# Preparing the weight tiles of seven-product pairs one pair ahead, in a two-layer streaming encoder

## The chip, the cores and the metric

The kernel runs on one core of one Trainium2 chip. The metric is the device time in microseconds (us) of one execution. The engines are TensorE (PE, with PEld for its weight loads), VectorE (DVE), ScalarE (ACT), GpSimd (POOL) and SyncE (SP, which here only issues DMA transfers). POOL computes a little and issues the transfers that add their source to their destination.

## The reference, cut to what matters

An encoder of two layers works on 576 tokens (512 of a prompt, 64 of a sample) of width 1024. Each layer is a feed-forward sub-layer, a token mixer and a second feed-forward sub-layer. Every sub-layer reads a norm whose shift and scale, and writes a residual whose gate, come from a conditioning vector `c`:

```python
for l in range(DEPTH):
    mod = (cond @ ada_w[l] + ada_b[l]).reshape(b, N_SUB, 3, D_MODEL)
    shift, scale, gate = mod[:, :, 0], mod[:, :, 1], mod[:, :, 2]
    hh = _modulated_norm(x, norm_g[l, 0], shift[:, 0], scale[:, 0])
    x = x + 0.5 * gate[:, 0, None] * _swiglu(hh, ff_w_in[l, 0], ff_w_out[l, 0])
    ...  # token mixer: gated delta rule and short convolution (l = 0), stick-breaking attention (l = 1)
    hh = _modulated_norm(x, norm_g[l, 2], shift[:, 2], scale[:, 2])
    x = x + 0.5 * gate[:, 2, None] * _swiglu(hh, ff_w_in[l, 1], ff_w_out[l, 1])

def _swiglu(h, w_in, w_out):
    gate, up = jnp.split(h @ w_in, 2, axis=-1)
    return (jax.nn.silu(gate) * up) @ w_out
```

`w_in` is 1024 x 5632 and `w_out` 2816 x 1024, all in float32. The four feed-forward sub-layers are called f0 to f3 here, the two mixers mixer 0 and mixer 1. The order is f0, mixer 0, f1, f2, mixer 1, f3.

## The kernel before

**Products in three matmuls.** Every operand is split into a high part (rounded to the matmul's float32r type) and a low part (what is left). A product is three matmuls: high x high, high x low, low x high. Activations lie in `XH`/`XL` (the sub-layer's input) and `HH`/`HL` (the hidden units), weights in `wh`/`wl`. Tokens are worked on in two halves of 288 columns.

**Weights** come from HBM in tiles of up to 128 x 1024 into a ring of three buffers named `stage`. ACT copies a tile to `wh`, and DVE (or POOL) writes `wl` = tile - `wh`. In other places `wl` is made without DVE: ACT writes `-wh` to `wl`, and a transfer issued by POOL adds the tile to it (`acc_dma`). `wh` and `wl` are rings of four buffers of 128 x 1024.

**Pairs.** A pair is one tile of gate and one of up columns (128 columns each). A plain pair takes 96 matmuls (2 tiles x 8 x 3 x 2 halves). In f1, f2 and f3 the last 16 of the 22 pairs are done with seven products of half-size blocks in place of eight (`dense7`): 84 matmuls, in seven steps of 12, in the order P1, P2, P6, P5, P7, P3, P4. P1, P6, P7 and P4 add to one PSUM bank, and ACT or DVE reads it between them, so that P6 cannot start before ACT has copied what P1 left (`sg`), nor P7 before the copy after P6. Each such pair needs four weight tiles:

- tile 0 (128 x 1024, the loaded tile `st[i, 0]` itself), for P1 and P2,
- tile 1 (128 x 1024, sums of loaded blocks made by DVE in `ss`), for P6 and P5,
- tile 2 (128 x 1024, more sums in `ss`), for P7 and P3,
- tile 3 (128 x 512, a loaded block), for P4.

`w_sum` makes the sums (four DVE operations a pair), `w_tile` calls `w_split` on one of the four. P5, P6, P7 and P4 also need sums of activation blocks, `TH`/`TL`, which `t_task` makes once a sub-layer: four ACT copies, a chain of eight adding transfers on POOL's queue, and four ACT and four DVE operations at its end.

**Order of the work.** Every engine takes its instructions in the order in which the program writes them. `dense7` writes, after the matmuls of each step, the work for other engines (`evac` and the `n ==` lines below them): sums and tiles of the next pair, too. Around them generators (`t_task`, `norm`, the attention's tasks and `ada_task`) are stepped when their due time has passed on a modelled clock (`Model`, `Sched`), so a constant in the model moves what is written where. `ada_task` makes the shift, scale and gate values: for each tile of `ada_w` a load of 512 KB (`aw`) and two DVE operations (`jk`), one tile every so many modelled ns. In f1 and f2 it has 48 tiles to do, every 11000 ns; in mixer 1 24 tiles, every 12000 ns, and the last step of mixer 1 (`last_pairs`) is written only after all of them (`S.finish(at)`).

**Where a sub-layer begins**, `start_sub` runs its first two pairs with the matmuls of both interleaved, while the norm of the second token half is still being made; `mid()` is called between the halves. Plain pairs 2 to 5 follow, then the seven-product pairs 6 and 7 and the first part of the `w_out` products; pairs 8 to 15 and the second part; pairs 16 to 21 and the last part.

Each instruction is recorded through one helper (line 191) or, for adding transfers, line 560, so the profile's groups are told apart by the names of their tiles.

## Time and profile before

| | |
|---|---|
| median of 3 runs | 2574.02 us (2572.0 to 2576.96) |
| the profiled execution | 2568.52 us, span 2566.8 us |
| PE busy | 2385.5 us (93%), mean granted clock 0.960 |
| DVE busy | 1702.3 us (66%) |
| ACT busy | 1050.9 us (41%) |
| POOL busy | 453.7 us (18%) |
| adding transfers to `wl` | 32 of 512 KB from `ss`, 32 of 256 KB from `stage` |

The page names PE as the busy engine, so what counts are the stretches in which it waits. PE matmuls are pipelined: one lasts some 300 ns, and at full clock one starts every 0.132 us. An idle time stands in square brackets with the instruction or transfer that ended it. "Landing" of a transfer is counted from the start of its issue to the arrival of its data.

### The profile page before, as it was taken

The page shows a single profiled execution, that of the slowest core. Times are in us where ns is not written, and L with a number is a line of the kernel's source. Part 1 is how long each engine was busy: PE and PEld are TensorE (multiplying, and loading weights), DVE is VectorE, ACT ScalarE, POOL GpSimd, SP SyncE. Part 2 cuts the span into 40 slices and gives each one's busy share as a digit, 9 for nine tenths or more (in the row PEclk, how much of TensorE's full clock was granted, in tenths as well). Part 3 has the DMA queues.
Part 4 walks back from the last instruction along what each step waited for, and adds up shares of the span by engine and source line. Part 5 has one row for each costly group of instructions (what it writes and reads, how often), then busy time and mean ns, then how long its engine had stood idle before and what let it go on. Part 6 is the DMA issues. An engine that isn't in the chain of part 4 may idle for free. (4 is left out here: it accounts for less than half of the span.)

```text
span 2566.8 us, 46156 instructions
## 1 busy us (share of the span) xinstructions
PE 2385.5 (93%) x18508; PEld 2301.0 (90%) x18508; DVE 1702.3 (66%) x3344; ACT 1050.9 (41%) x2090; POOL 453.7 (18%) x693
## 2 busy tenths in 40 slices
PE   7999999999998988989899999999999959899998
PEld 5999999988888988889899999999888849899998
DVE  7666666697875756686775546455777866648575
ACT  4322222533222433352544446264555535325352
POOL 4000000432222310010122001013334324000001
PEclk8999999998978999999999999999999979999999
DMA  6444443321112275574746446352333323623322
GB/s 234 159 155 147 155 150 118 115 81 51 46 49 90 84 199 161 139 200 150 198 139 165 117 103 161 94 143 85 126 118 120 98 85 123 165 84 98 99 81 81
DMA packets 108794, 318.84 MB, mean 124 GB/s; under 512 B 26226, under 2 KB 28530, under 8 KB 108324
## 3 DMA queue, kind: packets, MB, share of 16 engines
q1 hardware_dynamic: 95044, 273.02, 32.3%
q0 software_dynamic: 13536, 42.87, 9.1%
q8 instruction: 146, 2.39, 0.4%
q14 instruction: 68, 0.56, 0.1%
HBM read 261.47 MB, written 11.51 MB: 106 GB/s over the span
## 5 line engine op out<-in xcount | busy, mean ns | idle before, releaser
L191 PE MATMUL d<-XH,wh 128*128 128x288 f32 x2736 | 841.4, 308 | 52.5 <-DVE x L191 22.3
L191 PE MATMUL d<-XL,wh 128*128 128x288 f32 x2736 | 824.4, 301 | 11.4 <-POOL XL L191 9.9
L191 PE MATMUL d<-XH,wl 128*128 128x288 f32 x2736 | 822.6, 301 | 2.4 <-DVE wl L191 2.4
L191 PEld LDWEIGHTS d<-XH,wh 128*128 128x128 f32 x2736 | 528.2, 193 | 61.7 <-issue 26.2
L191 PEld LDWEIGHTS d<-XL,wh 128*128 128x128 f32 x2736 | 528.2, 193 | 23.4 <-POOL XL L191 16.3
L191 PEld LDWEIGHTS d<-XH,wl 128*128 128x128 f32 x2736 | 527.6, 193 | 3.8 <-DVE wl L191 3.5
L191 DVE TENSOR_TENSOR wl<-stage,wh 128x1024 fp32r<-128x1024 f32 (+3 forms) x287 | 331.1, 1159 | 193.4 <-ACT wh L191 191.7
L191 ACT ACTIVATE wh<-stage 128x1024 fp32r<-128x1024 f32 (+3 forms) x393 | 333.2, 867 | 247.4 <-PE d L191 229.2
L191 PE MATMUL d<-HH,wh 128*128 128x288 f32 x1408 | 416.4, 296 | 1.1 <-ACT HH L191 1.1
L191 PE MATMUL d<-HL,wh 128*128 128x288 f32 x1408 | 416.1, 296 | 0.1
L191 PE MATMUL d<-HH,wl 128*128 128x288 f32 x1408 | 414.2, 294 | 0.0
L191 DVE SCALAR_TENSOR_TENSOR jk<-aw,cb 128x1024 bf16<-128x1024 f32 x272 | 340.5, 1252 | 15.3 <-DMA aw<-in_ada 10.5
L191 DVE SCALAR_TENSOR_TENSOR x<-d,mod,x 128x64 f32<-128x64 f32 (+2 forms) x384 | 146.5, 412 | 227.8 <-PE d L191 227.0
L191 PE MATMUL d<-TH,wl 128*128 128x288 f32 x768 | 232.8, 303 | 44.0 <-DMA wl<-ss 44.0
L191 PEld LDWEIGHTS d<-HH,wh 128*128 128x128 f32 x1408 | 264.2, 188 | 1.3 <-ACT HH L191 1.3
L191 PEld LDWEIGHTS d<-HL,wh 128*128 128x128 f32 x1408 | 264.3, 188 | 1.0 <-DVE HL L191 1.0
L191 PEld LDWEIGHTS d<-HH,wl 128*128 128x128 f32 x1408 | 264.6, 188 | 0.0
L191 PE MATMUL d<-TH,wh 128*128 128x288 f32 x768 | 229.5, 299 | 6.6 <-ACT sg L191 6.6
L191 PE MATMUL d<-TL,wh 128*128 128x288 f32 x768 | 229.6, 299 | 0.0
L191 POOL TENSOR_TENSOR acc<-acc,sq 128x288 f32<-128x288 f32 x72 | 58.4, 811 | 847.9 <-ACT sq L191 847.3
L191 PEld LDWEIGHTS d<-TH,wl 128*128 128x128 f32 x768 | 147.5, 192 | 50.4 <-DMA wl<-ss 50.4
L191 ACT ACTIVATE HH<-hm 128x288 fp32r<-128x288 f32 x176 | 73.5, 442 | 253.4 <-DVE hm L191 252.6
(321 smaller groups left out, 3333.4 us busy)
## 6 DMA issues: line engine op xcount, KB each, us to landing
stage<-in_w SPq DMA_DIRECT2D x301, 512.0 KB, 3.6
aw<-in_ada SPq DMA_DIRECT2D x136, 512.0 KB, 3.7
wl<-ss POOLq DMA_DIRECT2D x32, 512.0 KB, 4.7
stage<-in_w SPq DMA_DIRECT2D x36, 384.0 KB, 3.1
TL<-XL POOLq DMA_DIRECT2D x18, 576.0 KB, 9.4
wl<-stage POOLq DMA_DIRECT2D x32, 256.0 KB, 5.2
TL<-XH POOLq DMA_DIRECT2D x6, 576.0 KB, 9.4
TL<-TL POOLq DMA_DIRECT2D x6, 576.0 KB, 5.6
```

The costliest lines, as they stand in the source:

```text
L191: r = real(*args, **kw)
```

## The change

Six edits:

1. In `dense7` tile 0 of the next pair is written after step P1 (it was after P5), tile 1 after P5 (was after P3), tile 2 after P3 (was after P4). Tile 3 of the running pair stays after P1 and is now always the only one left to do there, but for the first pair of a row, which still makes its tile 2 at that place.
2. Tile 3 gets its own buffers `wh3` and `wl3` (one each, 128 x 512), so a pair takes three of the four buffers of the ring and not all four.
3. Where adding transfers make `wl` (f1 and f2), they do it for tiles 0 and 3, which are loaded data. Tile 2, a sum, is now subtracted on DVE, as tile 0 was. The counts stay: 32 of 512 KB and 32 of 256 KB.
4. `t_task` is spawned in `mid()`, that is between the two halves of a sub-layer's first two pairs, and not behind them.
5. The model has a clock of its own for adding transfers (`ACC`, at 130 in place of 150 GB/s) beside that of the loads. `ada_task` in mixer 1 takes 8500 ns a tile and not 12000.
6. To make room, the ring `hf` of the norms has four buffers and not five, and `dynamic_dma_scratch_size` is 1024 and not 2048.

```diff
-        self.t = {"PE": 0.0, "DVE": 0.0, "ACT": 0.0, "POOL": 0.0, "SP": 0.0, "DMA": 0.0}
+        self.t = {"PE": 0.0, "DVE": 0.0, "ACT": 0.0, "POOL": 0.0, "SP": 0.0, "DMA": 0.0, "ACC": 0.0}
...
     def w_split(i, src, E=V, by_dma=False):
         n = Model.size(src)
-        h, l = wsp.tile([P, 1024], F32R, name="wh"), wsp.tile([P, 1024], F32R, name="wl")
+        if n == HB:
+            h, l = (wsp.tile([P, HB], F32R, name=m, bufs=1) for m in ("wh3", "wl3"))
+        else:
+            h, l = wsp.tile([P, 1024], F32R, name="wh"), wsp.tile([P, 1024], F32R, name="wl")
...
         if n == 0:
-            w_split(i, st[i, 0])
+            w_split(i, st[i, 0], by_dma=S2M[0])
         if n == 1:
             w_split(i, ss[i, 1])
         if n == 2:
-            w_split(i, ss.pop((i, 3)), by_dma=S2M[0])
+            w_split(i, ss.pop((i, 3)))
...
             if n == 0:
-                while len(wt[i]) < 4:
-                    if len(wt[i]) == 2:
-                        w_sum(i, 4)
-                    w_tile(i, len(wt[i]))
+                if len(wt[i]) < 3:
+                    w_sum(i, 4)
+                    w_tile(i, 2)
+                w_tile(i, 3)
             if nxt7:
                 for k in {1: (1,), 2: (2,), 4: (3, 4)}.get(n, ()):
                     w_sum(i + 1, k)
-                k = {3: 0, 5: 1, 6: 2}.get(n)
+                k = {0: 0, 3: 1, 5: 2}.get(n)
                 if k is not None:
                     w_tile(i + 1, k)
...
         nc.gpsimd.dma_start(out, in_, accum_op=OP.add)
         M.issue("POOL", [out], [in_], 1000.0)
-        M.t["DMA"] = max(M.t["DMA"], M.t["POOL"] + 1300.0) + 4.0 * P * Model.size(out) / 150.0
-        M.mark([out], [in_], M.t["DMA"] + 700.0, "POOL")
+        M.t["ACC"] = max(M.t["ACC"], M.t["POOL"] + 1300.0) + 4.0 * P * Model.size(out) / 130.0
+        M.mark([out], [in_], M.t["ACC"] + 700.0, "POOL")
...
-            u = pool.tile([P, 288], F32, name="hf", bufs=5)
+            u = pool.tile([P, 288], F32, name="hf", bufs=4)
...
-    def start_sub(task, evacs):
+    def start_sub(task, evacs, after=None):
 
         def mid():
             S.finish(task[1])
             hold[0] = False
+            if after:
+                after()
...
-                        start_sub(task, [ev0, evac])
-                    tt = S.spawn(t_task(pool)) if PLAIN[2 * l + s // 2] < 22 else None
+                        start_sub(task, [ev0, evac], lambda: tt.append(S.spawn(t_task(pool))))
                 elif seven(pos[0]):
                     if tt:
-                        S.finish(tt)
-                        tt = None
+                        S.finish(tt.pop())
...
-        at = S.spawn(ada_task(mp, [(1, j) for j in (5, 6, 7)], 12000.0, 1))
+        at = S.spawn(ada_task(mp, [(1, j) for j in (5, 6, 7)], 8500.0, 1))
...
-    nc = _bacc.Bacc("TRN2", target_bir_lowering=False, num_devices=1, dynamic_dma_scratch_size=2048)
+    nc = _bacc.Bacc("TRN2", target_bir_lowering=False, num_devices=1, dynamic_dma_scratch_size=1024)
```

**Place 1: a seven-product pair in f1, on ACT.** First ACT's order before, from the `up` copy (after P7) of one pair to the `hm` copy (after P5) of the next. `wh<-ss x2` and `wl<-ss` are tile 1 and tile 2, `wh<-stage 128x512` and its `wl` are tile 3; the first `sg<-d` is the copy after P1.

```order
L191 ACTIVATE up<-d 128x288
L191 ACTIVATE wh<-ss 128x512 x2
L191 ACTIVATE sg<-sg 128x288
L191 ACTIVATE wh<-ss 128x512 x2
L191 ACTIVATE wl<-ss 128x1024
L191 ACTIVATE sg<-d 128x288
L191 ACTIVATE wh<-stage 128x512
L191 ACTIVATE wl<-stage 128x512
L191 ACTIVATE HH<-hm 128x288 x2
L191 ACTIVATE sg<-d 128x288
L191 ACTIVATE hm<-d 128x288
```

And the same piece of the changed kernel (its numbered names are `wh3` and `wl3`):

```order
L191 ACTIVATE up<-d 128x288
L191 ACTIVATE wh<-ss 128x512 x2
L191 ACTIVATE sg<-sg 128x288
L191 ACTIVATE sg<-d 128x288
L191 ACTIVATE wh_11700<-stage 128x512
L191 ACTIVATE wl_11701<-stage 128x512
L191 ACTIVATE wh<-stage 128x512 x2
L191 ACTIVATE wl<-stage 128x1024
L191 ACTIVATE HH<-hm 128x288 x2
L191 ACTIVATE sg<-d 128x288
L191 ACTIVATE hm<-d 128x288
```

Tile 2's three ACT operations are gone from ahead of the copy after P1, and the next pair's tile 0 now stands between tile 3 and `HH`. On DVE the same pairs hold, before, two `ada_w` tiles a pair (`jk,mod`), and in the changed kernel one. Before:

```order
L191 TENSOR_TENSOR ss<-ss,stage 128x512
L191 TENSOR_TENSOR wl<-stage,wh 128x1024
L191 SCALAR_TENSOR_TENSOR jk,mod<-aw,cb 128x1024 x2
L191 TENSOR_TENSOR ss<-stage 128x512
L191 TENSOR_TENSOR ss<-stage,ss 128x512
L191 TENSOR_TENSOR up<-hm,up 128x288
L191 TENSOR_TENSOR sg<-d,sg 128x288
L191 TENSOR_TENSOR wl<-ss,wh 128x1024
L191 SCALAR_TENSOR_TENSOR jk,mod<-aw,cb 128x1024 x2
L191 TENSOR_TENSOR hm<-sg,up 128x288
```

In the changed kernel:

```order
L191 TENSOR_TENSOR ss<-ss,stage 128x512
L191 TENSOR_TENSOR wl<-ss,wh 128x1024
L191 SCALAR_TENSOR_TENSOR jk,mod<-aw,cb 128x1024 x2
L191 TENSOR_TENSOR ss<-stage 128x512
L191 TENSOR_TENSOR ss<-stage,ss 128x512
L191 TENSOR_TENSOR up<-hm,up 128x288
L191 TENSOR_TENSOR sg<-d,sg 128x288
L191 TENSOR_TENSOR wl<-ss,wh 128x1024
L191 TENSOR_TENSOR hm<-sg,up 128x288
```

So it is with most pairs of f1: the modelled clock runs slower per pair, and the `ada_w` tiles spread into the first pairs of f2. In four pairs of f1 the one tile stands where it stands here, between `wl` of tile 1 and the sums; in the others it stands elsewhere in the pair.

**Place 2: DVE where f1 enters its first seven-product pair.** `TL<-TL,TH` are the four last operations of `t_task`. Before:

```order
L191 TENSOR_TENSOR TL<-TL,TH 128x1152
L191 SCALAR_TENSOR_TENSOR jk,mod<-aw,cb 128x1024 x2
L191 TENSOR_TENSOR TL<-TL,TH 128x1152
L191 TENSOR_TENSOR hm<-sg,d 128x288
L191 TENSOR_TENSOR HL<-hm,HH 128x288
L191 TENSOR_TENSOR wl<-stage,wh 128x1024
L191 TENSOR_TENSOR hm<-sg,d 128x288
L191 TENSOR_TENSOR HL<-hm,HH 128x288
```

In the changed kernel:

```order
L191 TENSOR_TENSOR TL<-TL,TH 128x1152
L191 TENSOR_TENSOR hm<-sg,d 128x288
L191 TENSOR_TENSOR HL<-hm,HH 128x288
L191 TENSOR_TENSOR wl<-stage,wh 128x1024
L191 SCALAR_TENSOR_TENSOR jk,mod<-aw,cb 128x1024 x2
L191 TENSOR_TENSOR hm<-sg,d 128x288
L191 TENSOR_TENSOR HL<-hm,HH 128x288
L191 TENSOR_TENSOR ss<-stage 128x512
L191 TENSOR_TENSOR ss<-ss,stage 128x512
L191 TENSOR_TENSOR TL<-TL,TH 128x1152
```

The second `TL` operation has moved behind two token halves' worth of `hm` and `HL`; the transfers that it waits for are written earlier, too (edit 4).

**Place 3: DVE at the end of mixer 1**, from the last split of the attention's output to the residual of `last_pairs`. Before:

```order
L191 TENSOR_TENSOR XL<-so,XH 128x288 x6
L191 SCALAR_TENSOR_TENSOR jk,mod<-aw,cb 128x1024 x8
L191 TENSOR_TENSOR mod<-mod,small 128x16
L191 SCALAR_TENSOR_TENSOR mod<-mod,small 128x16
L191 TENSOR_TENSOR wl<-stage,wh 128x768 x2
L191 SCALAR_TENSOR_TENSOR x<-d,mod,x 128x288 x8
```

In the changed kernel:

```order
L191 COPY wt_23039<-a 64x128
L191 TENSOR_TENSOR XL<-so,XH 128x288 x6
L191 TENSOR_TENSOR wl<-stage,wh 128x768 x2
L191 SCALAR_TENSOR_TENSOR x<-d,mod,x 128x288 x8
```

The last four `ada_w` tiles, which stood ahead of the residual, have moved forward among the attention's work; the last of the 24 now stands ahead of the last attention pair's scans.

More of the change, by code (lines that the diff above doesn't have):

```diff
@@ L802, in ffn @@
         spool[0] = pool
-        tt = None
+        tt = []
         late = {}
@@ L880, in ffn @@
                     else:
-                        start_sub(task, [ev0, evac])
-                    tt = S.spawn(t_task(pool)) if PLAIN[2 * l + s // 2] < 22 else None
+                        start_sub(task, [ev0, evac], lambda: tt.append(S.spawn(t_task(pool))))
                 elif seven(pos[0]):
                     if tt:
-                        S.finish(tt)
-                        tt = None
+                        S.finish(tt.pop())
                     dense7(evac7(jj))
```

## The prediction

> **What bounds the kernel now.** PE is the busy engine, so I first read who makes it wait (columns: us in total, times, longest):
>
> ```profile
> PE d L191 <- DMA wl<-ss: 44.0, 26, 6.8
> PE d L191 <- DVE x L191: 22.3, 2, 19.7
> PE d L191 <- ACT wh L191: 15.6, 3, 7.3
> ```
>
> All three belong to this change: tile 2's adding transfer, the residual at the end of mixer 1, and the entry into the seven-product pairs. What they cost in full is read from stretches between the starts of P1, in the view by windows (us; then busy us and count of PE, PEld, DVE, ACT, POOL; clock; DMA share; GB/s). Three rows each for f1, f2 and f3: pairs 6 and 7 with the first `w_out` part, pairs 8 to 15 with the second, pairs 16 to 20; then six pairs of f3:
>
> ```profile
> 968.58:1053.13 84.55, 76.52 (x554) 75.84 (x553) 54.38 (x94) 25.47 (x45) 3.44 (x4) 0.94 0.47 144
> 1053.13:1217.73 164.60, 145.81 (x1059) 143.47 (x1057) 125.67 (x221) 73.97 (x144) 13.80 (x16) 0.98 0.64 179
> 1217.73:1286.91 69.18, 60.13 (x422) 58.85 (x421) 53.94 (x96) 39.30 (x82) 8.67 (x10) 0.95 0.72 189
> 1428.35:1505.81 77.46, 75.02 (x555) 74.78 (x554) 34.10 (x58) 25.12 (x43) 3.48 (x4) 0.98 0.37 102
> 1505.81:1653.92 148.11, 142.09 (x1058) 140.37 (x1057) 78.56 (x136) 73.28 (x144) 13.82 (x16) 1.00 0.50 129
> 1653.92:1716.99 63.07, 58.57 (x422) 57.40 (x421) 37.02 (x64) 40.25 (x84) 8.62 (x10) 0.97 0.60 144
> 2230.74:2307.12 76.38, 74.03 (x555) 73.33 (x553) 42.84 (x73) 22.11 (x39) 0.00 (x0) 1.00 0.28 83
> 2307.12:2447.14 140.02, 140.02 (x1058) 140.02 (x1057) 91.97 (x152) 61.66 (x128) 0.00 (x0) 1.00 0.30 91
> 2447.14:2502.81 55.67, 55.67 (x422) 55.67 (x421) 44.12 (x73) 32.09 (x72) 0.00 (x0) 1.00 0.30 93
> 2318.25:2385.05 66.80, 66.80 (x506) 66.80 (x505) 54.96 (x92) 39.88 (x90) 0.00 (x0) 1.00 0.31 95
> ```
>
> f3 is the yardstick: 66.80/6 = 11.13 us a pair, PE never idle, a step 11.13/7 = 1.59 us. Its second stretch less six pairs (140.02 - 66.80) is 73.2, the floor of the first. Over the floor lie: f1 11.3 + 24.6 + 13.5 = 49.4; f2 4.2 + 8.1 + 7.4 = 19.7; f3 3.2. Together 72.3 us.
>
> **Why a pair is slow now.** Rows of one f2 pair that starts at 1519.69, from the timeline (start, us, engine):
>
> ```profile
> 1520.19 1.04 ACT L191 ACTIVATE wl<-ss 128x1024 fp32r<-128x1024 f32 x1
> 1521.48 0.41 ACT L191 ACTIVATE sg<-d 128x288 f32<-128x288 f32 x1 [0.25 <-PE d L191]
> 1521.79 0.63 ACT L191 ACTIVATE wh<-stage 128x512 fp32r<-128x512 f32 x1
> 1522.31 0.62 ACT L191 ACTIVATE wl<-stage 128x512 fp32r<-128x512 f32 x1
> 1522.83 0.77 ACT L191 ACTIVATE HH<-hm 128x288 fp32r<-128x288 f32 x2
> 1526.90 1.14 ACT L191 ACTIVATE wh<-stage 128x512 fp32r<-128x512 f32 x2
> ...
> 1521.59 0.86 POOL L560 DMA_DIRECT2D wl<-ss  x1 [9.33 <-ACT wl L191]
> 1523.29 0.86 POOL L560 DMA_DIRECT2D wl<-stage  x1 [0.84 <-ACT HH L191]
> ...
> 1524.13 0.82 DVE L191 TENSOR_TENSOR HL<-hm,HH 128x288 fp32r<-128x288 f32 x2
> 1524.87 0.68 DVE L191 TENSOR_TENSOR ss<-ss,stage 128x512 f32<-128x512 f32 x1
> 1528.07 1.23 DVE L191 TENSOR_TENSOR wl<-stage,wh 128x1024 fp32r<-128x1024 f32 x1 [2.52 <-ACT wh L191]
> 1529.22 0.69 DVE L191 TENSOR_TENSOR ss<-stage 128x512 f32<-128x512 f32 x1
> 1529.82 0.69 DVE L191 TENSOR_TENSOR ss<-stage,ss 128x512 f32<-128x512 f32 x1
> ...
> 1105.90 1.22 DVE L191 SCALAR_TENSOR_TENSOR jk<-aw,cb 128x1024 bf16<-128x1024 f32 x1
> ```
>
> Two clocks run beside PE. One is the transfer: issue to landing takes, in f2 (first row) and f1 (second), min/median/max:
>
> ```profile
> DMA to landing us min/median/max: 4.4/4.9/5.9
> DMA to landing us min/median/max: 4.6/6.2/7.8
> ```
>
> P7 wants tile 2 at 4 x 1.59 = 6.4 us after the pair's start. Issued at 1.9 (1521.59) and landed 4.4 to 4.9 later it is there at 6.3 to 6.8; each us that ACT comes later, PE waits.
>
> The other is a loop through ACT and DVE, from one copy after P1 (the first `sg<-d`, 1521.48) to the next. Counted from it in these rows: `HL` begins at 2.7, the sum behind it ends at 4.1, tile 0's `wh` begins at 5.4 (ACT had P5's copy ahead of it), its `wl` ends at 7.8, the last sums at 9.0. Then DVE's two subtractions after P3 (0.75), ACT's `silu` (0.35) and tile 2 (`wh` 1.1, `wl` 1.0): the next copy at 12.2. f2's second stretch has 8.1/8 = 1.0 over 11.13, 12.1 a pair. In f1 the order has two `ada_w` tiles a pair, each two operations like the last row, 2.4 us, and the first lies inside the loop: 14.6; measured are 24.6/8 = 3.1 over, 14.2. So in f1 this loop sets the pace, in f2 it and the transfer do.
>
> **The change: seven-product pairs (edits 1 to 3).** Counts per pair stay, so only places matter. New loop on ACT from the copy after P1, s: 0.3 + 0.5 + 0.5 (tile 3) + 1.05 + 0.95 (tile 0) + 0.75 (`HH`) = 4.1. DVE: `HL` and sum, to s + 5.7. ACT: tile 1's `wh` to 6.9; DVE: its `wl` to 8.1, sums to 9.4; ACT: tile 2's `wh` to 10.5, `silu` to 10.85, next copy. That is under 11.13: without `ada_w` PE sets the pace again. With one `ada_w` tile between `wl` and the sums it is 10.85 + 2.4 = 13.3, 2.1 over; at the pairs where it stands by `HL` or `wh` it is partly covered (about 1); behind `hm` wholly.
>
> The new transfer: tile 3 is issued at 3.6 as now; tile 0's ACT ends at 5.2, its issue is at 5.6, and landing takes 4.9, up to 5.9 in f2: 10.5 to 11.5. Needed at the third matmul of the next P1, 11.13 + 0.26 = 11.4. In time, just. In f1 6.2 gives 11.8; but half the `ada_w` loads per pair are gone there, and late copies (the 13.3 case) delay the next P1 anyway. What P7 waits for in its place: the copy after P6 ends at about 6.3, against 6.4. I take 0.15 for such pairs.
>
> Row starts: P7 of pairs 8 and 16 gets tile 2 from DVE at about 4.7, not from a transfer; I leave 1 each. At pairs 6 of f1 and f2 the order puts two `TL` operations (1.36 each by DVE's rows below) and an `ada_w` tile ahead of tile 2's sum: P7 waits 2 to 3, the next P1 2, so 5; f3 1.5.
>
> Left over the floor: f1 5.5 for the entry, 10.7 for pairs 8 to 15 (three at 2.1, one at 1.3, two at 0.9, start 1, two at 0.15), 9.1 for 16 to 20 (three at 2.1, 1.3, start 1, 0.5): 25.3; f2 5 + 3.5 (one at 2.1) + 1.5 = 10; f3 1.5; together 36.8. Saved: 72.3 - 36.8 = **35.5**. Bounds: 72 if loop and transfer bind nowhere; 25 less if tile 0 lands 7.8 after issue everywhere (13.4 - 11.4 = 2 a pair, in the some 13 pairs where nothing else is late).
>
> **Entry (edits 4 and 5).**
>
> ```profile
> 912.02 1.04 POOL L560 DMA_DIRECT2D TL<-XL  x1 [11.22 <-issue]
> ...
> 2215.22 1.36 DVE L191 TENSOR_TENSOR TL<-TL,TH 128x1152 fp32r<-128x1152 f32 x1 [8.01 <-DMA TL<-TL]
> ...
> 956.85 0.61 PE L191 MATMUL d<-XH,wh 128*128 128x288 f32 x1 [7.27 <-ACT wh L191]
> ...
> 1416.16 0.40 PE L191 MATMUL d<-XH,wh 128*128 128x288 f32 x1 [1.39 <-ACT wh L191]
> ...
> 2218.41 0.61 PE L191 MATMUL d<-XH,wh 128*128 128x288 f32 x1 [6.93 <-ACT wh L191]
> ...
> 953.67:960.50 6.83, 3.23 (x12) 2.89 (x13) 5.32 (x8) 3.73 (x8) 0.86 (x1) 0.50 0.72 178
> 2216.60:2223.40 6.80, 4.58 (x17) 4.23 (x18) 5.26 (x10) 2.66 (x6) 0.00 (x0) 0.50 0.51 94
> ```
>
> DVE stands before a `TL` operation until the chain of adding transfers has gone far enough; `hm`, then `HH` and `wh` on ACT, queue behind it, and PE waits for that `wh`. POOL was idle 11.2 us before the chain's first issue (912.02): the issue can come when POOL's norm work is done (900.8) and the `TL` copies have begun, at about 901.5, 10.5 earlier. That alone covers 7.27 and 6.93, and DVE's second operation is written two half pairs later besides. PE runs at half clock for 3.65 and 5.0 us behind the two long waits, a loss of 1.8 and 2.5. Sum 7.3 + 1.4 + 6.9 + 4.3 = 19.9, and I take **20**, nothing for the ACT copies (4.3 us in the middle of a pair whose PE waits for the norm) and for `hf`, which with a buffer less lets DVE run four and not five steps ahead of POOL in a norm; neither is shown by a row, so both lie inside the bound: 0 to 22.
>
> The Trainium skill ("TensorE: Matmul & The Clock Gate", part 1, "What's actually happening") has the half clock follow an idle window of about 3.4 us; the trace agrees here, with waits of 7 us. By it the remaining waits of 1 to 3 us would cost no clock.
>
> **End of mixer 1 (edit 5).**
>
> ```profile
> 2117.31 0.58 PE L191 MATMUL d<-XH,wh 128*128 128x288 f32 x1 [19.73 <-DVE x L191]
> ...
> 2100.22 1.22 DVE L191 SCALAR_TENSOR_TENSOR jk<-aw,cb 128x1024 bf16<-128x1024 f32 x1 [3.34 <-DMA aw<-in_ada]
> ...
> 2117.30:2121.00 3.70, 3.69 (x15) 3.70 (x16) 1.66 (x4) 2.08 (x5) 2.40 (x3) 0.50 0.67 266
> ```
>
> Four `ada_w` tiles, each loaded only after the last, hold the residual, and PE has no PSUM bank left. In the changed order none is left there: 19.7 and half of 3.7 at half clock, **21.6**. The moved tiles now lie among attention work; each costs at most 2.4 if on its path, four of them 10.
>
> **Sum.** 35.5 + 20 + 21.6 = 77.1, from the span of 2566.8: 2489.7. The profiled execution was 1.7 longer than its span (2568.5), and the median of the runs (2574.0) is 5.5 above that execution: **2497**.
>
> **Rivals.** (a) *The loop does not bind*: DVE has slack enough (54.96 of 66.80 busy in f3), residue 6 and not 37: 2497 - 31 = 2466. For it: f3's loop runs at 11.13 with more DVE work. Against: f1's 14.2.
> (b) *Tile 0 lands late*: a wait at P1 for one at P7. Price 25 to 30 by the bound above: 2525. For it: f1's 7.8; against: half the `ada_w` loads.
> (c) *Mixer 1 gives it back*: the denser tiles cost 10, as above, and the norm that now follows sooner 5 (the wait in front of f3 besides the 19.7 is 22.3 - 19.7 = 2.6, doubled): 2512. For it: the attention's DVE work is on PE's path in mixer 1; against: 20 of the 24 tiles lie among that work already.
> (d) *Slower*: the halved scratch makes an adding transfer's issue wait until the one before has landed. Tile 3 lands at 8.0 (3.6 + 4.4), so tile 0 would be issued there and land at 12.6 to 13.9, 1.2 to 2.5 late in some 30 pairs: 55. The chain's eight transfers, in a row at 5.6 to 9.4 each (medians of the page), would end at 901.5 + 75 = 976 at the worst, against pair 6 at about 957 and P6 3 later: 16 a sub-layer, 48. Together 103: 2600. It turns to slower once these cost more than the 77 saved. For it: only the edit itself; against: three `TL` issues stand back to back in 2.6 us now.
>
> ```profile
> 935.92 2.64 POOL L560 DMA_DIRECT2D TL<-XL  x3 [6.33 <-DMA TL<-XH]
> ```
>
> The Trainium skill ("DMA: Bandwidth & Descriptors", "Terms") gives 16 bytes a descriptor, so by it 1024 bytes would hold 64; no run here shows it.
> (e) *Nothing changes*, each wait replaced by its like: 2574.
>
> **Chances.** Forecast 0.52 (its own bounds 2480 to 2512), (a) 0.17, (b) 0.13, (c) 0.11, (d) 0.05, (e) 0.02. To hold 8 in 10 the range takes in (a), (c) and (b): 2462 to 2540. A measurement tells 0.2% (5 us) from nothing: faster 0.93, same 0.02, slower 0.05.
>
> **What would show it.** Right: no PE wait for `wl<-ss`; f2's second stretch at 140 to 144; f1's at 150 to 153, with `ada_w` at its slow pairs; no wait over 3 us at pair 6 or in `last_pairs`. Wrong: `wl<-stage` as PE's largest wait (b), POOL issues spaced by landings (d), f1 at 140 (a), longer attention (c).

## The result, and the profile after

| | before | after |
|---|---|---|
| median of the runs shown with the result | 2573.01 us (4 runs) | 2497.07 us (4 runs, 2492.8 to 2500.48) |
| ratio | | 0.9708 (0.9679 to 0.9737) |
| profiled execution | 2568.52 us, span 2566.8 | 2500.48 us, span 2498.8 |
| PE busy, mean granted clock | 2385.5 us, 0.960 | 2381.8 us, 0.965 |

The kernel is 76 us faster by the medians, 68 us by the two profiled executions. Single executions of one kernel lie up to 0.9% from its median (2549.85 us against 2573.17 in one set of the kernel before), so what follows is read from stretches of the profiles. How well these repeat is seen in three traces whose pairs are those of the kernel before (before, and the runs `room_only` and `mix_8500_only` below): a single stretch differs by up to 2.3 us, the excess of all pairs is 72.3, 73.5 and 72.4 us, that of the three entries 23.7, 25.5 and 27.2.

Who makes PE wait in the changed kernel (the waits of PE; us in total, times, longest):

```profile
PE d L191 <- ACT sg L191: 17.1, 18, 5.0
PE a L191 <- DVE sg L191: 16.7, 28, 2.0
PE a L191 <- DVE cp L191: 6.9, 8, 2.7
PE d L191 <- DVE x L191: 2.8, 2, 2.6
```

No row names `wl<-ss` any more (44.0 before), `ACT wh` (15.6) is gone, and the residual's wait fell from 22.3 to 2.8. New at the top is `sg`, the copy between P1, P6 and P7; the attention's waits (PSUM tile `a`) grew from 11.4 and 4.8 to 16.7 and 6.9.

The view by windows of the changed kernel, for the stretches that the prediction shows of before (pairs 6 and 7, pairs 8 to 15, pairs 16 to 20 of f1 and f2; of f3 the first, the others are within 0.5 us of before), then the three entries, from the norm's last wait to the start of pair 6:

```profile
962.88:1043.36 80.48, 75.30 (x555) 74.84 (x554) 53.45 (x90) 27.38 (x45) 3.48 (x4) 0.98 0.50 151
1043.36:1189.04 145.68, 143.01 (x1058) 140.43 (x1057) 109.59 (x193) 74.06 (x144) 13.91 (x16) 1.00 0.65 178
1189.04:1249.77 60.73, 57.90 (x423) 55.98 (x422) 47.93 (x84) 39.69 (x82) 8.70 (x10) 1.00 0.76 191
1385.07:1466.16 81.09, 75.83 (x554) 75.36 (x553) 53.29 (x89) 27.37 (x45) 3.48 (x4) 0.96 0.50 150
1466.16:1607.68 141.52, 140.94 (x1058) 140.20 (x1057) 81.91 (x144) 73.86 (x144) 13.89 (x16) 1.00 0.54 135
1607.68:1664.11 56.43, 56.22 (x422) 55.75 (x421) 37.37 (x64) 40.49 (x84) 8.68 (x10) 1.00 0.70 159
2162.34:2238.94 76.60, 74.02 (x554) 73.32 (x553) 40.58 (x68) 23.49 (x40) 0.00 (x0) 1.00 0.27 83
...
904.76:962.88 58.12, 58.12 (x437) 58.12 (x438) 35.48 (x52) 22.11 (x36) 9.65 (x11) 1.00 0.87 220
1326.94:1385.07 58.13, 58.13 (x438) 58.13 (x439) 35.46 (x52) 22.11 (x36) 9.52 (x11) 1.00 0.87 220
2104.22:2162.34 58.12, 58.12 (x438) 58.12 (x438) 40.56 (x60) 21.87 (x36) 8.57 (x10) 1.00 0.87 229
```

The same three entries before, from the same view of the kernel before:

```profile
900.86:968.58 67.72, 60.03 (x437) 59.46 (x438) 37.61 (x54) 25.52 (x39) 8.83 (x10) 0.95 0.75 189
1366.04:1428.35 62.31, 60.19 (x438) 59.73 (x439) 29.68 (x41) 25.89 (x39) 8.71 (x10) 0.97 0.69 163
2162.76:2230.74 67.98, 60.64 (x437) 60.06 (x438) 38.21 (x55) 25.88 (x39) 8.67 (x10) 0.95 0.76 196
```

An entry without a wait takes 58.1 us. With this and the prediction's floors of 73.2, 140.0 and 55.7 for the stretches, the 68.0 us between the two spans divide so:

| place | over its floor before | after | saved | forecast |
|---|---|---|---|---|
| seven-product stretches f1, f2, f3 | 49.4, 19.7, 3.2 | 18.0, 10.1, 3.9 | 40.3 | 35.5 |
| the three entries | 9.6, 4.2, 9.9 | 0, 0, 0 | 23.7 | 20 |
| mixer 1 (start of f2's pair 21 to f3's entry) | | | 5.7 | 21.6 |
| from f1's pair 21 to f2's entry | | | 2.0 | |
| from f3's pair 21 to the end | | | 0.3 | |
| all that lies before f1's entry | | | -3.9 | |

The last line is 900.86 against 904.76, the ends of a part that the change hardly touches; over all traces of this case it ends between 900.5 and 907.6.

### The profile page after: what moved, and what is told of

The parts are those of the page before. It is cut to its first block, busy times and chain, and to the rows that moved or that the text cites. A ratio compares the mean times of both kernels' runs of the same rounds, so it can differ in the third digit from the quotient of the medians.

```text
span 2498.8 us, 46134 instructions
## 1 busy us (share of the span) xinstructions
PE 2381.8 (95%) x18508; PEld 2297.1 (92%) x18508; DVE 1708.8 (68%) x3344; ACT 1057.8 (42%) x2090; POOL 461.6 (18%) x693
## 5 line engine op out<-in xcount | busy, mean ns | idle before, releaser
L191 DVE TENSOR_TENSOR wl<-stage,wh 128x1024 fp32r<-128x1024 f32 (+3 forms) x255 | 292.6, 1154 | 135.7 <-ACT wh L191 133.8
L191 PE MATMUL d<-TH,wh 128*128 128x288 f32 x768 | 229.4, 299 | 18.4 <-ACT sg L191 16.7
L191 PE MATMUL d<-TH,wl 128*128 128x288 f32 x768 | 227.6, 296 | 0.0
L191 POOL TENSOR_TENSOR acc<-acc,sq 128x288 f32<-128x288 f32 x72 | 58.1, 807 | 828.6 <-ACT sq L191 828.0
L191 PEld LDWEIGHTS d<-TH,wh 128*128 128x128 f32 x768 | 145.4, 189 | 24.3 <-ACT sg L191 22.0
```

The costliest lines, as they stand in the source:

```text
L191: r = real(*args, **kw)
```

## The experiments

Twelve more kernels were run, each timed beside the kernel before. Where a run is compared with the changed kernel, the latter is taken at its 2497 us, which was not measured again beside it.

### The room that was made

Kernel before, with edit 6 alone:

```diff
-name="hf", bufs=5        dynamic_dma_scratch_size=2048
+name="hf", bufs=4        dynamic_dma_scratch_size=1024
```

> The kernel before with edit 6 alone (hf four buffers, scratch 1024). My theory, that neither binds: within 5 us of before (2568 to 2578), issues of TL transfers still back to back. Rival (d), that an adding transfer waits for the one before it to land: slower by 20 us or more, POOL's three TL issues spaced by several us.

Measured: 2573.94 us, ratio 1.0006 (0.998 to 1.0032). Edit 6 costs nothing that shows, and rival (d) falls at its price. Its mechanism is there in a small way; rows of POOL in the timeline of this run, from f1 and from f2:

```profile
940.37 1.73 POOL L560 DMA_DIRECT2D TL<-XL  x2 [6.49 <-DMA TL<-XH]
944.15 0.88 POOL L560 DMA_DIRECT2D TL<-XL  x1 [2.04 <-issue]
...
1406.13 0.86 POOL L560 DMA_DIRECT2D TL<-XL  x1 [1.02 <-DMA TL<-XL]
```

Before, the prediction's row had three such issues back to back (`x3`, 2.64 us). Here the third waits 2.04 us. In f1 the profile names nothing that it waits for, but in f2 it names the landing of an earlier transfer, and the landings of f1 fit: the transfer issued at 933.02 lands 10.8 us later, at 943.84, and the held issue follows after 0.31 us. The same gap of 0.30 to 0.31 us stands at this place in all three sub-layers, here and in the changed kernel, always behind the landing of the third transfer before it. So a fourth transfer of 576 KB is not issued here while three are under way; in the kernel before four were (the one issued at 936.99 while that of 928.74, which lands at 939.37, was still out). Rival (d) had the wait behind one transfer, it is behind three. The pairs of 256 KB and 512 KB transfers never come to three and are not held up.

### The order of the tiles, alone

Kernel before, with edits 1, 2, 3 and 6 (no edit 4, no edit 5).

> The kernel before with edits 1, 2, 3 and 6, without the earlier t_task, the model's own clock for adding transfers and the 8500 ns. The order has 1.4 ada_w tiles a pair in f1, where it had 2. My theory (the placing itself frees the pairs): no PE wait for wl<-ss, f2's pairs at 11.1 to 11.5 us, f1's at 12.5 to 13, together 28 to 35 us saved, 2538 to 2546; the entry's waits of 7 us stay. Rival (most of the saving in the pairs comes from spreading the ada_w tiles): less than 15 us saved.

Measured: 2522.33 us, ratio 0.9826 (0.9796 to 0.9855), 45 us less by this ratio and 51 by the medians, more than the 28 to 35 that I expected; its profiled execution, 2532 us, was the second slowest of five, and its span is 36.3 us under before's. The excess of all pairs is 31.9 us here and 32.0 in the full change, so edits 1 to 3 alone make that gain: 40.4 us. It is spread otherwise: the stretches with pair 6 are 10.9 us over here and 18.6 in the full change, which moves `TL` operations into pair 6; f1's later pairs are 19.5 over here and 10.7 there, with 19 `ada_w` tiles in them here and 13 there. Edits 4 and 5 thus give and take 8 us in the pairs. The entries came out at 67.7, 67.3 and 68.0, 5.0 more than before, all of it in f2, little beyond the 3.5 by which traces of the same pairs differ; that PE reaches the same late `TL` operations sooner there is likely and not shown.

### The adding transfers back on the sums

The changed kernel without edit 3:

```diff
-            w_split(i, st[i, 0], by_dma=S2M[0])
+            w_split(i, st[i, 0])
...
-            w_split(i, ss.pop((i, 3)))
+            w_split(i, ss.pop((i, 3)), by_dma=S2M[0])
```

> The changed kernel without edit 3: tile 2 (a sum) by the adding transfer again, tile 0 by DVE, everything else as changed. My theory: tile 2's low part costs ACT 1.0 us more inside the loop (10.85 + 1.0, over 11.13), and its transfer, issued some 2.5 us after the next pair's start, lands at 7 to 7.5 where P7 wants it at 6.4: f2's pairs at about 12, PE waits for wl<-ss again, 15 to 30 us slower than the changed kernel, 2512 to 2527. Rival (a pair ahead is enough for either tile): within 5 us of the changed kernel.

The order by due times puts one `ada_w` tile less ahead of f1's first residual here, so that residual reads its gate before the gate's last tile is in, and the values that this kernel computes from there on are wrong. It does the same amount of work, so it is used here for its time alone.

Measured: 2532.71 us, ratio 0.9837 (0.9805 to 0.9869), 36 us above the changed kernel, where 15 to 30 was expected and the rival had at most 5. Its waits of PE, and the second stretches of f1 and f2:

```profile
PE d L191 <- DMA wl<-ss: 32.9, 23, 3.8
...
1039.35:1200.47 161.12, 147.17 (x1059) 143.66 (x1058) 112.04 (x195) 74.30 (x144) 13.87 (x16) 0.98 0.60 164
1488.52:1639.05 150.53, 144.71 (x1058) 143.31 (x1057) 81.53 (x142) 73.75 (x144) 13.87 (x16) 0.98 0.50 126
```

f2's pairs are back at 10.5 us over 140.0, slower than before the change (8.1). The excess of all pairs is 68.8 of before's 72.3 us: preparing a pair ahead saves 3.5 us without edit 3, and 40.3 with it. In both orders that were run, the transfer that follows two sums comes too late and the one that follows a load does not. (Edit 3 without edits 1 and 2 was not tried. In this run ACT also does tile 2's third operation inside the loop again, 1.04 us in the rows of before; how much of the 36 us is that was not separated.)

### What the entry owes to which edit

Kernel before, with edit 4 alone (`t_task` spawned in `mid()`):

> The kernel before with edit 4 alone. My theory: the waits of 7 us in front of the first seven-product pairs of f1 and f3 go, 17 to 24 us saved, 2549 to 2556, the pairs themselves as before (14 us in f1). Rival (the first seven-product pair takes back what the entry gains, since PE comes sooner to tiles that are as late as before): less than 10 us.

Measured: 2575.36 us, ratio 1.0002 (0.9982 to 1.0022): nothing. The rival's bound holds, but not for its reason. DVE's rows in the timeline of this run, then PE's row, and the three entries by windows:

```profile
945.02 1.36 DVE L191 TENSOR_TENSOR TL<-TL,TH 128x1152 fp32r<-128x1152 f32 x1 [5.85 <-DMA TL<-TL]
946.30 0.45 DVE L191 TENSOR_TENSOR hm<-sg,d 128x288 f32<-128x288 f32 x1
...
946.80 0.61 PE L191 MATMUL d<-XH,wh 128*128 128x288 f32 x1 [9.60 <-DVE hm L191]
...
907.59:976.87 69.28, 59.67 (x438) 59.44 (x439) 38.76 (x55) 22.77 (x37) 8.77 (x10) 0.93 0.73 184
1370.57:1440.14 69.57, 60.42 (x437) 60.19 (x438) 32.07 (x45) 22.97 (x37) 8.60 (x10) 0.93 0.65 154
2174.93:2246.10 71.17, 61.00 (x437) 60.25 (x438) 42.38 (x62) 22.66 (x37) 8.56 (x10) 0.93 0.74 187
```

The transfers do start earlier, but DVE's `TL` operations are written earlier still, three half pairs ahead of where they stood. DVE stands in front of one (5.85 us), `hm` queues behind it, and PE waits 9.60 us where it had waited 7.27. The entries got 12.1 us longer in all, and the stretches with pair 6 got 8.3 shorter.

Why earlier still: `t_task` puts an operation into the program when the modelled landing of its transfers is past. The model before has one clock for loads and adding transfers, on which each queues behind the one written ahead of it. Edit 5 gives the adding transfers a clock of their own and a lower rate: a `TL` transfer, 4 x 128 x 1152 bytes, takes 4.5 us by it and 3.9 before, where the page has 9. So the next run took this part of edit 5 alone:

```diff
-        M.t["DMA"] = max(M.t["DMA"], M.t["POOL"] + 1300.0) + 4.0 * P * Model.size(out) / 150.0
-        M.mark([out], [in_], M.t["DMA"] + 700.0, "POOL")
+        M.t["ACC"] = max(M.t["ACC"], M.t["POOL"] + 1300.0) + 4.0 * P * Model.size(out) / 130.0
+        M.mark([out], [in_], M.t["ACC"] + 700.0, "POOL")
```

> Edit 5's model clock for adding transfers, alone, in the kernel before; nothing else changes. Edit 4 alone saved nothing: its first seven-product pairs and its t_task were written earlier, but the model, which lets adding transfers run at 150 GB/s beside the loads, also wrote the TL operations earlier (two of them three half pairs sooner), so that DVE stood 5.9 us in front of the second and PE 9.8 us behind it. Theory A (the entry's gain comes from the two together, t_task earlier and the TL operations not): here the chain of transfers still starts at 912 but its TL operations are written two half pairs later, so PE's waits of 7.3, 1.4 and 6.9 us shrink, and part of them comes back at pair 6, where the last two TL operations now stand: 2 to 5 us saved an entry. Beside it the ada_w tiles of f1 fall from two a pair to one: f1's excess of 49 us over its floor falls by 8 to 12, f2's rises by 1 to 2. In all 12 to 22 us under before. Theory B (the model's clock does nothing for the entry): only the ada_w tiles, 5 to 10 us.

And one took the clock together with edit 4 (and with an `ada_w` tile every 10600 modelled ns in f1 and f2, not 11000):

> Edit 4 and edit 5's model clock together in the kernel before (ada_w tiles in f1 and f2 every 10600 modelled ns and not 11000, so that the eighth of f1's gate is still done when f1 first reads it). Theory A (the two together make the entry's gain): the waits of 7.3, 1.4 and 6.9 us and the half clock behind them are gone, 18 to 22 us; f1's ada_w tiles are one a pair, 8 to 12; pair 6 of f1 and f2 takes two TL operations and so 2 to 6 more each. Under before by 20 to 30 us, and under edit 4 alone by as much. Theory B (the entry's gain needs the new order of the tiles): 5 to 12 us under before, the long waits still there.

Measured: the clock alone 2558.82 us, ratio 0.9946 (0.9925 to 0.9967); both 2550.51 us, 0.9919 (0.9899 to 0.9939). With the clock alone all three entries are at 58.1 us already. Its rows of PE in pair 6 of f1 show where part of that went:

```profile
966.14 0.40 PE L191 MATMUL d<-TL,wh 128*128 128x288 f32 x1 [2.28 <-DVE TL L191]
977.12 0.61 PE L191 MATMUL d<-TH,wl 128*128 128x288 f32 x1 [5.64 <-DMA wl<-ss]
```

The last `TL` operations now stand in pair 6, and tile 2's transfer waits behind them.

Which half of this edit counts can be read from the order in which the program is written. In f1 of the kernel before the four `TL` operations stand 165, 147, 69 and 51 matmuls ahead of pair 6. With the rate of 130 alone, on the shared clock, they stand in the same four places; with a clock of their own at the old 150 they stand 120, 12, 0 and 0 ahead; with both, as in the run, 90, 0, 0 and 0. The `ada_w` tiles of f1's pairs 8 to 15 thin out with the clock of their own at either rate, and not with the rate alone. So it is the separate clock that moves the work, and the rate adds to it. A likely reason is that loads modelled behind ten adding transfers hold up the modelled PE, so that few matmuls are written before a task is due. (The orders with one half alone were not timed.)

Excess in us over the floors, from the starts of P1 and the norm's last waits:

| kernel | three entries | three stretches with pair 6 | sum |
|---|---|---|---|
| before | 23.7 | 18.7 | 42.4 |
| edit 4 alone | 35.8 | 10.4 | 46.2 |
| model clock alone | 0 | 30.0 | 30.0 |
| both (tiles every 10600 ns) | 0 | 17.1 | 17.1 |
| full change | 0 | 18.6 | 18.6 |

So the entry's gain is the model clock's; edit 4 is worth 13 us more once the clock is there (the chain ends before pair 6), and costs 4 without it. Two parts of my expectations missed: the clock alone clears the entry wholly, not by 2 to 5 us each, and one `ada_w` tile a pair in f1 in place of two was worth little (the stretches after pair 6 fell from 38.1 to 34.0 us with the clock, and stood at 39.1 with both), presumably because there the transfer of tile 2 still sets the pace.

The same from the other side, the changed kernel without that clock:

> The changed kernel without the part of edit 5 that gives adding transfers their own clock in the model (all else as changed). By the runs so far the entry's gain is this model clock and not the earlier t_task: the clock alone took the whole excess of the three entries (23.7 us over 58.1 each), edit 4 alone made them longer (35.8), since it let the model write two TL operations three half pairs ahead of their data. Theory A (what counts is where the TL operations stand on DVE): they stand here where they stand with edit 4 alone, so the entries lie 11 to 13 us each over 58.1, 33 to 39 in all, with one PE wait of 9 to 10 us each; pair 6 gets 8 to 14 us back, since no TL operation stands in it any more; f1's pairs hold 1.5 ada_w tiles and not 1, 3 to 5 us. In all 23 to 32 over the changed kernel, 2520 to 2529. Theory B (with the new tile order a late TL operation on DVE hides behind work that is now done earlier): 0 to 8 over it.

Measured: 2532.0 us, ratio 0.983 (0.979 to 0.9869), 35 us above the changed kernel by the medians and 30.4 by the two spans, where 23 to 32 was expected. PE's rows, f1 and f2:

```profile
942.93 0.61 PE L191 MATMUL d<-XH,wh 128*128 128x288 f32 x1 [9.61 <-DVE hm L191]
...
1384.86 0.61 PE L191 MATMUL d<-XH,wh 128*128 128x288 f32 x1 [11.16 <-DVE hm L191]
```

The entries are 37.4 us over, the stretches with pair 6 gave 12.3 back, both as expected; f1's pairs from 8 on, with 19 `ada_w` tiles in place of 13, cost 10.7 more, not 3 to 5: 1.8 us for each tile more, of the 2.4 that it takes.

### Pair 6 of f1 and f2

In the changed kernel pair 6 takes 18.4 us in f1 and 19.0 in f2, where 11.1 is the floor. Rows of DVE, then ACT, then PE, from its timeline:

```profile
965.18 2.63 DVE L191 TENSOR_TENSOR TL<-TL,TH 128x1152 fp32r<-128x1152 f32 x2 [0.60 <-ACT TH L191]
967.72 1.22 DVE L191 SCALAR_TENSOR_TENSOR jk<-aw,cb 128x1024 bf16<-128x1024 f32 x1
970.13 0.69 DVE L191 TENSOR_TENSOR ss<-stage,ss 128x512 f32<-128x512 f32 x1
...
970.86 0.63 ACT L191 ACTIVATE wh<-ss 128x512 fp32r<-128x512 f32 x1 [3.84 <-DVE ss L191]
974.42 0.39 ACT L191 ACTIVATE sg<-d 128x288 f32<-128x288 f32 x1
...
974.86 0.43 PE L191 MATMUL d<-TH,wh 128*128 128x288 f32 x1 [4.87 <-ACT sg L191]
```

P7 waits for `sg`; that copy stands on ACT behind tile 2's `wh`, which waits 3.84 us for tile 2's last sum, which stands on DVE behind two `TL` operations and an `ada_w` tile. If that is the cause, the sum written a pair earlier cures it:

```diff
                 w_sum(i, 3)
                 w_tile(i, 1)
+                w_sum(i, 4)
             return
...
                 if len(wt[i]) < 3:
-                    w_sum(i, 4)
                     w_tile(i, 2)
```

> The changed kernel with the fourth sum of a row's first seven-product pair written in the pair before, ahead of the TL operations and the ada_w tile. In the changed kernel P7 of pairs 6 of f1 and f2 waits 5.0 and 5.1 us for ACT's copy after P6, which queues behind tile 2, which waits for this sum. My theory: these waits fall to about 1, 6 to 10 us saved, 2487 to 2491. Rival (ACT's queue of tiles 2, 3 and 0 behind P1 is what holds the copy): less than 3 us.

Measured: 2487.4 us, ratio 0.9664 (0.9637 to 0.969), 10 us under the changed kernel. Pair 6 takes 13.4 and 13.5 us, and P7's longest wait there is 0.92 us.

### The `ada_w` tiles in f1's pairs

The changed kernel, with no `ada_w` tile inside f1's and f2's seven-product pairs (`ada_task` waits while `hold[0]` is set) and one every 5000 modelled ns elsewhere:

```diff
         nxt7 = seven(i + 1)
+        hold[0] = S2M[0]
...
         wt.pop(i)
+        hold[0] = False
...
-        at = S.spawn(ada_task(ap, [(0, 8)] + [(1, j) for j in range(5)], 11000.0))
+        at = S.spawn(ada_task(ap, [(0, 8)] + [(1, j) for j in range(5)], 5000.0))
```

> The changed kernel, in which ada_task in f1 and f2 pauses during seven-product pairs and takes 5000 ns a tile elsewhere: no ada_w tile lies between the steps of a seven-product pair. The same 48 tiles are made. My theory (the loop through ACT and DVE with an ada_w tile in it sets the 12.4 us of f1's pairs): f1's pairs fall to 11.1 to 11.5, 10 to 16 us saved against the changed kernel, 2481 to 2487. Rival (the DVE time is paid wherever the tiles go, or f1's pairs are slow for the loads' sake): within 4 us of the changed kernel.

Measured: 2496.59 us, ratio 0.9701 (0.9667 to 0.9735): no difference from the changed kernel. The windows of f1 in this run, and PE's rows in pair 6:

```profile
963.15:1054.31 91.16, 80.72 (x554) 79.70 (x553) 71.81 (x119) 29.13 (x49) 4.25 (x5) 0.91 0.58 170
1054.31:1195.51 141.20, 140.68 (x1058) 140.14 (x1057) 102.80 (x181) 73.81 (x144) 13.87 (x16) 1.00 0.65 171
1195.51:1252.88 57.37, 56.47 (x422) 55.76 (x421) 39.09 (x68) 40.43 (x84) 8.68 (x10) 1.00 0.74 174
...
966.84 0.61 PE L191 MATMUL d<-XH,wl 128*128 128x288 f32 x1 [3.27 <-DMA wl<-stage]
975.78 0.40 PE L191 MATMUL d<-TH,wh 128*128 128x288 f32 x1 [3.29 <-ACT sg L191]
```

Both theories were half right. f1's later stretches fell by 7.8 us to 1.2 and 1.7 over their floors, so 7.8 of their 10.7 us of excess in the changed kernel are the `ada_w` tiles. But six tiles (2.4 us of DVE each) now stand between 953.9 and 979.8, around the last `TL` operations, and pair 6 paid 10.7 us. DVE's time was paid at the one place where the tiles pile up, and the last run below tells whether it must be.

### Mixer 1

Two runs take edit 5's other half in and out:

```diff
-        at = S.spawn(ada_task(mp, [(1, j) for j in (5, 6, 7)], 12000.0, 1))
+        at = S.spawn(ada_task(mp, [(1, j) for j in (5, 6, 7)], 8500.0, 1))
```

The kernel before with 8500:

> The kernel before with 8500 ns a tile in mixer 1 alone. In the trace of the changed kernel the stretch of mixer 1 saved 6 us, not the 21.6 forecast: the wait of 19.7 was gone, but the attention took some 10 us more by matmul 2500 of the stretch. Theory A (the moved ada_w tiles cost that on DVE, always): 4 to 9 us saved, 2564 to 2569. Theory B (the attention's loss was chance or came with the other edits): 15 to 24 us saved, 2549 to 2558.

The changed kernel with 12000:

> The changed kernel with 12000 ns a tile in mixer 1, as before. Theory A (the moved tiles cost most of what the late wait cost): 4 to 9 us slower than the changed kernel, 2501 to 2506, with a PE wait of some 20 us ahead of the residual of last_pairs. Theory B: 15 to 24 us slower, 2512 to 2521.

Measured: 2559.77 us, ratio 0.9953 (0.9927 to 0.9978), and 2505.54 us, ratio 0.9728 (0.9697 to 0.9759), 8 us above the changed kernel. The first falls between its two theories (13 us under the kernel before by the medians), the second is what theory A says. From the start of f2's pair 21 to f3's entry the kernel before takes 445.8 us and 437.8 with 8500; the changed kernel takes 440.1, and 445.6 with 12000. How this comes about is seen by comparing the start of the same matmul, counted from pair 21 on. Just ahead of the residual, at matmul 2664, 8500 ns leaves the kernel before 12.5 us behind where it is with 12000, and the changed kernel 15.0 behind; at matmul 2700, past the residual, the two are 9.1 and 6.7 ahead. So the residual gives 21.6 and 21.7 us, and the attention work ahead of it gives back 12 to 15. Rows of the changed kernel, DVE and PE, and a window:

```profile
1955.26 1.21 DVE L191 SCALAR_TENSOR_TENSOR jk<-aw,cb 128x1024 bf16<-128x1024 f32 x1
1958.57 1.20 DVE L191 TENSOR_TENSOR_SCAN cp<-sn,ones 128x448 f32<-128x448 f32 x1
...
1964.86 0.54 PE L191 MATMUL d<-XH,wh 128*128 128x288 f32 x1 [1.52 <-ACT XH L191]
1967.31 0.61 PE L191 MATMUL d<-XL,wh 128*128 128x288 f32 x1 [1.91 <-DVE XL L191]
...
1961.55:1964.96 3.41, 1.72 (x12) 1.28 (x10) 1.33 (x5) 2.66 (x9) 0.92 (x3) 1.00 0.01 3
1964.96:1971.79 6.83, 4.92 (x22) 2.85 (x23) 6.79 (x14) 3.84 (x11) 0.00 (x0) 0.50 0.00 0
```

An `ada_w` tile stands in front of the scans of a long attention row, PE has nothing else to do and waits for the split behind them, and its clock is halved for 6.83 us. This is one such place; the 15 us were not traced to single rows.

### A version from these parts

The sum a pair earlier, no `ada_w` tile in the seven-product pairs of f1 and f2 but one every 7000 modelled ns elsewhere, and 10000 ns in mixer 1:

> The changed kernel with three edits: a row's first pair gets its last sum (w_sum 4) in the pair before (this alone saved 10 us); no ada_w tile is written within f1's and f2's seven-product pairs, and elsewhere one every 7000 modelled ns, so that 10 and not 14 stand before pair 6 of f1; and mixer 1 takes a tile every 10000 ns, so that the last attention work keeps the order that it has with 12000 but no tile is left for the residual. Theory A (each stall has its own cause and they add): pair 6 8 us less in all as measured, f1's pairs 8 less (as with the tiles held, whose f1 pairs ran at 11.1), of which the earlier pairs give back up to 3; mixer 1's attention back at the pace it has with 12000, 10 less, less up to 2.4 for each of the last four tiles: 4 to 10. So 18 to 27 under the changed kernel: 2470 to 2479. Theory B (DVE's work is paid wherever it stands): only the 10 us of the sum, 2485 to 2490.

Measured: 2472.33 us, ratio 0.9607 (0.9579 to 0.9635), 25 us under the changed kernel. Its windows of f1, and f2's first:

```profile
958.93:1035.48 76.55, 73.76 (x554) 73.32 (x553) 56.43 (x97) 27.17 (x45) 3.48 (x4) 1.00 0.59 174
1035.48:1177.11 141.63, 140.89 (x1058) 140.18 (x1057) 95.56 (x164) 73.77 (x144) 13.91 (x16) 1.00 0.62 161
1177.11:1233.76 56.65, 56.48 (x422) 55.80 (x421) 36.93 (x65) 40.49 (x84) 8.70 (x10) 1.00 0.67 150
...
1369.03:1448.52 79.49, 75.14 (x554) 74.69 (x553) 58.00 (x99) 27.26 (x45) 3.48 (x4) 0.98 0.57 175
```

All pairs together are 16.6 us over their floors (32.0 in the changed kernel), and mixer 1 to f3's entry is 10.9 us shorter. This lies in theory A's range, so the gains add, and DVE's time is mostly not paid where the tiles now stand. The largest piece left sits in f2's pair 6 (6.3 over).

## Why the prediction was right, and where not

The time was met: 2497 forecast, 2497.07 measured. That the two agree within 0.1 us is luck. Against the span, to which the sum was made, the forecast was 77.1 us and the profile shows 68.0: mixer 1 gave 15.9 less than forecast, the pairs and the entries 8.5 more, parts without a forecast took 1.6. The 9 us that were missing came back because the medians fell further than the two profiled executions: 77.0 us from the 2574.02 on which the forecast was built. The range of 2462 to 2540 took in the times of three rivals as well, so the number alone says little for the mechanism.

Of the signs that the prediction named, two came as said: no PE wait for `wl<-ss`, and f2's second stretch at 141.5 (140 to 144). Two did not: f1's second stretch came out at 145.7 and not at 150 to 153, and P7 of pair 6 waits 4.87 us where no wait over 3 was to be. Two signs of being wrong showed: longer attention (c) and, at one place of the `TL` chain, issues spaced by landings (d).

**Pairs: right in kind, 4.8 us too little** (35.5 against 40.3). The transfer of tile 0 in time was the point with the least room, and it held: in the pairs that run at the floor it is issued 5.6 to 5.7 us after the pair's start and lands 5.3 us later (the page's median), 10.9 to 11.0 against 11.4; PE's waits for `wl<-stage` are two, 0.7 us in all. P7's new 0.15 us wait for the copy did not show in f2's pairs at the floor (11.14 us); in the slow pair of f1 below, P6 waits 0.17 us and P7 0.56. The loop with an `ada_w` tile between `wl` and the sums was forecast at 13.3 us and takes 12.4. Its rows, ACT and DVE of an f1 pair in the changed kernel:

```profile
1070.10 0.39 ACT L191 ACTIVATE sg<-d 128x288 f32<-128x288 f32 x1
...
1074.64 0.68 DVE L191 TENSOR_TENSOR ss<-ss,stage 128x512 f32<-128x512 f32 x1
1076.54 1.23 DVE L191 TENSOR_TENSOR wl<-ss,wh 128x1024 fp32r<-128x1024 f32 x1 [1.22 <-ACT wh L191]
1077.68 1.22 DVE L191 SCALAR_TENSOR_TENSOR jk<-aw,cb 128x1024 bf16<-128x1024 f32 x1
1080.10 0.69 DVE L191 TENSOR_TENSOR ss<-stage 128x512 f32<-128x512 f32 x1
...
1080.82 0.63 ACT L191 ACTIVATE wh<-ss 128x512 fp32r<-128x512 f32 x1 [3.97 <-DVE ss L191]
```

From the copy at 1070.10 the sum behind `HL` ends at 5.2 and not 5.7, and ACT begins tile 2's first half at 10.7, when the first of the two sums is ready; I had it wait for both. These are the two mis-sized terms of the loop. By place, f1 was forecast at 25.3 over its floors and came to 18.0, f2 at 10 and came to 10.1, f3 at 1.5 and came to 3.9. Against the gain in f1's later pairs, pair 6 was forecast at 5 us over in f1 and f2 and 1.5 in f3, and was 7.3, 7.9 and 3.4: the right rows (two `TL` operations, an `ada_w` tile) and the right wait, taken as 2 to 3 us where it is 4.9, with 3.41 us at half clock behind it (975.10 to 978.51).

**Entry: right size, wrong cause.** 20 against 23.7 us. The step that failed is that the earlier issue "alone covers 7.27 and 6.93": the issue did come earlier, at 904.65 where 901.5 was forecast, but by itself it makes the wait longer (9.60). What I had put as "written two half pairs later besides" is all of it, and it comes from edit 5's clock, to which the sum gave no price of its own.

**Mixer 1: mis-sized, 5.7 for 21.6 us.** The residual's gain came as forecast: against the kernel before the changed kernel is 14.7 us behind at the last matmul ahead of the residual and 6.9 ahead behind it, which makes 21.6. The step that failed is that the sum put the moved `ada_w` tiles at nothing: the attention ahead of the residual takes 14.7 us longer, and the last 1.2 are lost on the way to f3's entry. That is rival (c), priced at 15 in all, to which I had given 0.11 on the ground that 20 of the 24 tiles lay there already. They did, but with 12000 ns they happened to lie beside the path, and 8500 puts one in front of the scans, as the rows above show; the order of those rows was there to be read. One sentence more fell: the Trainium skill ("TensorE: Matmul & The Clock Gate", part 1, "What's actually happening") has the half clock follow an idle window of about 3.4 us, and I had concluded that waits of 1 to 3 us would cost no clock. The window at 1964.96 has 0.50, and in the 3.41 us ahead of it PE is busy for 1.72 and idle for 1.69. The trace of the kernel before shows it too: behind a wait of 2.78 us (1062.71) the clock is halved for 3.41 us.

**Of the rivals**, (a) is half real: without `ada_w` tiles f1's pairs do run at the floor, as the runs with the tiles held show. (b) has no wait of note (the 0.7 us above). (d) cost nothing that shows; its sum also counted eight transfers of the `TL` chain where each sub-layer issues ten (30 in all by the page), as does the text on `t_task`. (c) happened, inside the forecast, and half of it was balanced by the other two terms. (e) is out.

## What to carry to other kernels

Put the slow way of making a tile (here an adding transfer, 5 us) on the operand whose source is ready first, and the quick way on the one that is ready last; here that choice, with the order that it needs, made 37 of the 40 us. Where a modelled clock decides what is written when, it matters which transfers share a clock in the model and how fast they run there: moving a task's start without mending that put DVE in front of data that was not there. Filler work costs anything between nothing and its time (1.8 of 2.4 us a tile in f1's pairs), depending on the row that it stands ahead of, so read that row before it is spread more densely.

## What was not expected of the hardware

With half the scratch size a fourth 576 KB adding transfer was issued only 0.30 to 0.31 us after the first of the three ahead of it had landed (2.04 us late in `room_only`, 3.31 in the changed kernel at 930.84).

The granted clock halves for stretches of 3.41 us or a multiple of it (3.41 to 17.07 in the changed kernel from f1's entry on; one more is cut by the end of the program), and no single wait needs to be that long. All eight such stretches there follow 3.41 us in which PE is idle for at least 1.64 us in all. Of the pieces of the same 3.41 us grid behind which the full clock went on, PE was idle for at most 1.34 us, but for one with 1.70 (all by the matmul ends that the profile models). In the kernel before the two groups overlap (halved from 1.47 us on, not halved up to 1.82). So in these two traces the mark lies at about half of 3.41 us, and what decides within the overlap is open, as is why single executions of one kernel differ by up to 0.9%.
